# Rotary embedding: the half swap by DMA in place of a product with a sign matrix

## The chip, the cores and the metric

The kernel runs on one core of one Trainium2 chip. Five engines work beside each other, each through its own instructions in order: TensorE (PE in the profile) for matrix products, VectorE (DVE), ScalarE (ACT), GpSimd (POOL) and SyncE (SP), which here issues most of the DMAs. ACT and POOL issue some DMAs too. Tiles live in SBUF; matrix products go to PSUM. The metric is the device time of one execution in microseconds, as the median over several runs.

## What is computed

Two transformer blocks over 256 tokens of width 1024. The first has a convolution and Fourier mixer, attention over a memory and a mixture of experts. The second has two layers, each a mixer and an MLP; the change lies in its two mixers alone. Cut to what matters:

```python
def apply_rope(t, cos, sin):
    t1, t2 = jnp.split(t, 2, axis=-1)            # 64 wide: two halves of 32
    rot = jnp.concatenate([-t2, t1], axis=-1)
    return (t * cos + rot * sin).astype(t.dtype)

def mixer_ab(h, cos, sin, w_in, q_norm, w_uq, w_uiq, sinks, w_out):
    aq, ak, av, cq, bk, bv, bik, biw = _split_widths(h @ w_in, AB_WIDTHS)
    ...    # rope of aq and ak (8 and 2 heads), window attention
    cq = rms_norm(cq, q_norm)
    ...    # rope of bq = cq @ w_uq, biq = cq @ w_uiq, bk and bik
    yb = dsa_attention(bq, bk, bv, biq, bik, iw)   # top 64 keys by index scores
    return jnp.concatenate([ya, yb], axis=-1) @ w_out

def mixer_c(h, cos, sin, w_in, w_out):
    q, k, v = jnp.split(h @ w_in, 3, axis=-1)
    ...    # rope of q and k, 16 heads, causal attention
    return moba_attention(q, k, v) @ w_out
```

## The kernel before

Features stand on the partitions and tokens along a row, so a head of 64 takes 64 partitions and two heads a tile of 128. The half swap of rope is then a move across partitions: row `f` needs row `f + 32` with a minus sign, or row `f - 32`.

`rope()` takes a projection in PSUM (`pA`) and cuts it into pieces of 128 x 2 x 256, called raws below. ACT copies each piece to an SBUF tile `raw`, of which there are two. A function `rotate`, put off to the next `tick` or `drain`, multiplies `raw` on PE with the constant sign matrix `rot` into a PSUM tile `pB`; POOL writes `raw` times cosine to the result, DVE writes `pB` times sine over `raw`, and DVE adds the two.

There are 16 pieces. `mixer_ab` has four calls of two: `kd` (all keys), `iq` (index queries), `bq` and `aq` (queries of its two attentions). `mixer_c` has four groups of four heads, and each calls `rope` for `q` (the tile `cq__` with a number) and `k` (`ck`), one piece each.

Around them: matrix products are made of three terms (lines L394 to L396) from weights that are split into a high and a low part, `wh` by ACT (L192) and `wl` by DVE (L195). The weights come in 1 MB and 2 MB loads on SP's queue into rings of buffers, and a load can start when the split of the one before in its slot is done. In `mixer_ab`, `select` makes the index scores of 8 heads (`scores`, L1353 and L1354), ACT applies a relu to `rl`, DVE adds them up weighted in `acc` (L1479) and takes the top 64 in 8 rounds (MAX and MATCH_REPLACE). In the meantime PE works on `uq` and `ab_in`, the projections of `bq` and `aq`. In `mixer_c` the attention of a group runs along with the projections of the next: S and its softmax on DVE and ACT, its scaling on POOL (L1394), transposes on PE (L479), `PT` copies on ACT (L1405). `ada` products for the next norm are spread through both as fillers (`adasb`, L615 to L627, `mods`).

The order of each engine's instructions is fixed when the program is built: a scheduler goes by its own estimates of durations, and each engine then works its list in order, waiting on semaphores.

Of the kernel before, what the change touches and what calls it, by code (L numbers as in the profile page):

```python
# [17 lines left out]
T, D, E, FF = 256, 1024, 32, 4096  # L18
# [19 lines left out]
C_ID, C_UP, C_ROT, C_CAUS, C_WIN, C_IOTA, C_INV, C_ONES, C_SEL, C_SLOT, C_END = (  # L38
    0, 128, 256, 384, 768, 1152, 1216, 1217, 1345, 1346, 1347)
# [3 lines left out]
def constants():  # L43
    p = np.arange(128)
    c = np.zeros((128, C_END), np.float32)
    c[:, C_ID:C_UP] = np.eye(128)
    c[:, C_UP:C_ROT] = p[:, None] < p[None, :]
    for f in range(128):
        if f % 64 < 32:
            c[f + 32, C_ROT + f] = -1.0  # L50
        else:
            c[f - 32, C_ROT + f] = 1.0
# [159 lines left out]
class Net:  # L212
# [269 lines left out]
    def setup(self, ld):  # L482
# [11 lines left out]
        self.rot = cst[:, C_ROT:C_CAUS]  # L494
# [6 lines left out]
        self.slot = cst[:, C_SLOT:C_END]  # L501
# [76 lines left out]
    def angles(self, rp):  # L578
# [10 lines left out]
        for dst, turn in ((self.sin, 0.0), (self.cos, 0.25)):  # L589
# [10 lines left out]
            nc.scalar.activation(dst, r, AF.Sin)  # L600
# [816 lines left out]
    def mixer_ab(self, p, h, extra):  # L1417
# [28 lines left out]
        self.rope(p, pk, kd)  # L1446
# [16 lines left out]
        self.rope(p, self.fm_block("uiq", 0, cq, 2), iq)  # L1463
# [31 lines left out]
        self.rope(p, self.fm_block("uq", 0, cq, 2), bq)  # L1495
        self.rope(p, self.fm_block("ab_in", 0, h), aq)
# [181 lines left out]
```

## Time and profile before

| | us |
|---|---|
| median of 3 runs (lowest to highest) | 1852.88 (1852.48 to 1853.91) |
| the profiled execution | 1858.61 |
| its span, first to last instruction | 1856.8 |
| PE busy | 1729.1 |
| DVE busy | 940.0 |
| ACT busy | 565.0 |
| POOL busy | 141.8 |

Busy times are sums over one profiled execution, on engines that work at the same time. The mean granted clock of TensorE in it is 0.979 of full speed. A row of the trace gives an instruction with the line of the kernel, what it writes and reads, and in brackets how long its engine was idle ahead of it and which instruction ended the wait. Buffer numbers are left out of names, so `pB` stands for many PSUM tiles.

### The profile page before, as it was taken

How to read it: one execution, taken by the hardware profiler on the slowest of the kernel's cores; microseconds unless marked ns; L12 is line 12 of the kernel's file. 1: busy time of each engine (PE TensorE's matmuls, PEld its weight loads, DVE VectorE, ACT ScalarE, POOL GpSimd, SP SyncE). 2: the span in 40 equal slices, each digit the busy share in tenths (PEclk: the TensorE clock that was granted, in tenths of full speed). 3: DMA queues.
4: the chain of work that ended last, by engine and by line, in shares of the span. 5: the costliest groups of instructions: out<-in, count | busy, mean ns of one | idle time of the engine just before them, and what ended most of it. 6: DMA issues, size and time to landing. Idle time of an engine off the chain costs nothing. (4 is left out here: it accounts for less than half of the span.)

```text
span 1856.8 us, 24948 instructions
## 1 busy us (share of the span) xinstructions
PE 1729.1 (93%) x10060; PEld 1110.4 (60%) x10060; DVE 940.0 (51%) x1752; ACT 565.0 (30%) x1037; POOL 141.8 (8%) x113
## 2 busy tenths in 40 slices
PE   7999999999989989899899988898999989989997
PEld 7998844434433333333333333665899978869996
DVE  6777413232322323132222223578877699977555
ACT  6445421111111111111111110437444444544442
POOL 0000000000000000000000000223300033330001
PEclk9999999999999999999999999899999999999999
DMA  8685879999999999999999999836477748536540
GB/s 313 225 309 205 342 307 422 425 424 425 425 424 427 424 425 424 425 425 425 427 423 427 424 426 378 272 131 243 162 279 263 247 157 260 204 114 237 194 159 24
DMA packets 133492, 588.17 MB, mean 317 GB/s; under 512 B 13110, under 2 KB 37148, under 8 KB 100604
## 3 DMA queue, kind: packets, MB, share of 16 engines
q1 hardware_dynamic: 131756, 581.28, 79.7%
q0 software_dynamic: 1328, 4.72, 0.8%
q8 instruction: 81, 1.33, 0.3%
q10 hardware_dynamic: 288, 0.52, 0.1%
q14 instruction: 39, 0.32, 0.0%
HBM read 585.45 MB, written 1.05 MB: 316 GB/s over the span
## 5 line engine op out<-in xcount | busy, mean ns | idle before, releaser
L195 DVE TENSOR_TENSOR wl<-wa,wh 128x1024 fp32r<-128x1024 f32 (+1 forms) x244 | 304.6, 1260 | 138.8 <-ACT wh L192 133.8
L192 ACT ACTIVATE wh<-wa 128x1024 fp32r<-128x1024 f32 (+1 forms) x246 | 250.5, 1031 | 252.5 <-PE pA L395 114.6
L1067 PE MATMUL pA<-wb,xT 128*64 128x512 f32 x1024 | 236.2, 601 | 20.1 <-DMA wb<-in_w_gate_up_dram 19.4
L390 DVE SCALAR_TENSOR_TENSOR ydl<-pB,slotw,ydh 128x512 fp32r<-128x512 f32 x32 | 24.0, 750 | 340.2 <-ACT ydh L389 340.2
L1039 ACT ACTIVATE xT<-pB,vp 128x128 f32<-128x128 f32 x128 | 40.0, 363 | 483.8 <-PE pB L1036 483.8
L1067 PEld LDWEIGHTS pA<-wb,xT 128*64 128x64 f32 x1024 | 68.7, 137 | 162.2 <-issue 113.5
L395 PE MATMUL pB<-hTh,wl 128*128 128x256 f32 x528 | 149.2, 283 | 1.5 <-DVE wl L195 1.5
L394 PE MATMUL pB<-hTh,wh 128*128 128x256 f32 x528 | 149.0, 282 | 1.2 <-ACT hTh L683 1.2
L396 PE MATMUL pB<-hTl,wh 128*128 128x256 f32 x528 | 148.8, 283 | 1.1 <-DVE hTl L685 1.1
L1132 DVE TENSOR_TENSOR x<-pB,x 128x512 f32<-128x512 f32 x128 | 79.7, 683 | 132.2 <-PE pB L1130 132.2
L1093 DVE TENSOR_TENSOR v<-pB,bgu 128x256 f32<-128x256 f32 x128 | 48.1, 418 | 180.2 <-PE pB L479 180.2
L1067 PE MATMUL pA<-wa,xT 128*64 128x512 f32 x528 | 125.5, 600 | 1.0 <-DMA wa<-in_w_gate_up_dram 1.0
L396 PE MATMUL pA<-hTl,wh 128*128 128x256 f32 x384 | 111.4, 291 | 7.8 <-DVE hTl L685 7.5
L394 PE MATMUL pA<-hTh,wh 128*128 128x256 f32 x384 | 115.5, 301 | 1.5 <-ACT hTh L683 1.0
L1111 PE MATMUL pB<-wa,aT 128*64 128x512 f32 x496 | 114.5, 596 | 0.3 <-DMA wa<-in_w_down_dram 0.3
L395 PE MATMUL pA<-hTh,wl 128*128 128x256 f32 x384 | 111.1, 290 | 0.3 <-DVE wl L195 0.3
L627 DVE SCALAR_TENSOR_TENSOR adasb<-wa,silu,adasb 128x512 f32<-128x512 f32 x126 | 106.6, 846 | 1.8
L394 PE MATMUL pA<-wh,amh 128*128 128x512 f32 (+1 forms) x272 | 103.6, 381 | 0.0
L396 PE MATMUL pA<-wl,amh 128*128 128x512 f32 (+1 forms) x272 | 102.9, 378 | 0.0
L395 PE MATMUL pA<-wh,aml 128*128 128x512 f32 (+1 forms) x272 | 102.7, 378 | 0.0
L394 PEld LDWEIGHTS pB<-hTh,wh 128*128 128x128 f32 x528 | 100.0, 189 | 3.3 <-ACT hTh L683 2.8
L395 PEld LDWEIGHTS pB<-hTh,wl 128*128 128x128 f32 x528 | 100.1, 189 | 2.7 <-DVE wl L195 2.3
(357 smaller groups left out, 3037.6 us busy)
## 6 DMA issues: line engine op xcount, KB each, us to landing
wb<-in_w_gate_up_dram SPq DMA_DIRECT2D x64, 2048.0 KB
wa<-in_w_gate_up_dram SPq DMA_DIRECT2D x66, 1024.0 KB
wa<-in_mlp_w_dram SPq DMA_DIRECT2D x64, 1024.0 KB
wa<-in_w_down_dram SPq DMA_DIRECT2D x62, 1024.0 KB
wa<-in_ada_w_dram SPq DMA_DIRECT2D x48, 1024.0 KB
wb<-in_w_down_dram SPq DMA_DIRECT2D x21, 2048.0 KB
wd<-in_w_gate_up_dram SPq DMA_DIRECT2D x20, 2048.0 KB
wc<-in_w_gate_up_dram SPq DMA_DIRECT2D x11, 2048.0 KB
```

The lines of the kernel that those rows point to most:

```text
L192: nc.scalar.activation(h, a, AF.Copy)
L195: eng.tensor_tensor(l, a, h.bitcast(F32), OP.subtract)
L390: nc.vector.scalar_tensor_tensor(lo, src, scale, hi.bitcast(F32), op0=OP.mult, op1=OP.subtract)
L394: mm(out, lh, rh, start=start, stop=False, skip_group_check=True)
L395: mm(out, ll, rh, start=False, stop=False, skip_group_check=True)
L396: mm(out, lh, rl, start=False, stop=stop, skip_group_check=True)
L627: nc.vector.scalar_tensor_tensor(sb, v, c, sb, op0=OP.mult, op1=OP.add)
L1039: nc.scalar.activation(xT[:, k, :n], ps[:, j, :n], AF.Copy, scale=g[:, k:k + 1])
L1067: self.up = nc.tensor.matmul(gu[h * 64:h * 64 + 64, b, :], xT[:, k, c0:c0 + SLOTS], w[0][:, n:n + 512], start=k == 0, stop=k == 7)
L1093: nc.vector.tensor_tensor(v[:, :, h, :], ps.rearrange("p (j h s) -> p j h s", j=4, h=2)[:, :, h, :], bias[:, h * 8 + b * 4:h * 8 + b * 4 + ...
L1111: self.up = nc.tensor.matmul(dn[h * 64:h * 64 + 64, :], aT[:, k, :], w[0][:, h * 512:h * 512 + 512], start=k == 0, stop=k == 7)
L1132: nc.vector.tensor_tensor(xs, ps, xs, OP.add)
```

## The change

The sign matrix and its product are gone. ACT copies a piece from PSUM straight into its place in the result tile. Four DMAs, issued by ACT, copy its four blocks of 32 partitions to the partitions 32 away into a second tile: in `mixer_c` a tile `turned` of which there are two, in `mixer_ab` a part of one of the two `S` buffers of the attention (`shared`). POOL multiplies the piece by the cosine in place, DVE multiplies the turned one by the sine in place, and DVE adds them. The minus sign sits in the sine: its activation has a scale of -1 or +1 for each partition. There are 64 such DMAs of 64 KB.

```diff
--- before.py
+++ after.py
...
+    c[:, C_SIGN] = np.where(p % 64 < 32, -1.0, 1.0)
...
@@ -597,7 +593,10 @@
             if turn:
                 nc.vector.tensor_scalar(r, r, math.pi / 2, None, op0=OP.add)
             nc.vector.tensor_scalar(r, r, 3.1415925, -3.1415925, op0=OP.min, op1=OP.max)
-            nc.scalar.activation(dst, r, AF.Sin)
+            if turn:
+                nc.scalar.activation(dst, r, AF.Sin)
+            else:
+                nc.scalar.activation(dst, r, AF.Sin, scale=self.sign)
             yield
@@ -1325,26 +1324,29 @@
                         out(n, z, mv[:, t, 0:1], rs[:, t:t + 1])
         return finish
 
-    def rope(self, p, ps, out):
+    def rope(self, p, ps, out, shared=False):
 
         nc = self.nc
         nb = ps.shape[1]
-        raw = p.tile([128, 2, T], F32, name="raw", bufs=2)
-        raws = [raw]
-        for j in range(0, nb, 2):
-            if j:
-                raws.append(p.tile([128, 2, T], F32, name="raw", bufs=2))
-            nc.scalar.activation(raws[-1], ps[:, j:j + 2, :], AF.Copy)
+        raws = [out[:, j:j + 2, :] for j in range(0, nb, 2)]
+        for j, raw in enumerate(raws):
+            nc.scalar.activation(raw, ps[:, 2 * j:2 * j + 2, :], AF.Copy)
+        if shared:
+            turned = p.tile([128, 4, 384], F32, name="S", bufs=2)[:, :nb, :T]
+        else:
+            turned = p.tile([128, nb, T], F32, name="turned", bufs=2)
+        for j, raw in enumerate(raws):
+            for i in range(4):
+                a, b = i * 32, (i ^ 1) * 32
+                nc.scalar.dma_start(turned[a:a + 32, 2 * j:2 * j + 2, :], raw[b:b + 32])
         sinb, cosb = (x[:, None, :].to_broadcast([128, 2, T]) for x in (self.sin, self.cos))
 
         def rotate():
             for i, raw in enumerate(raws):
-                r = self.B()
-                nc.tensor.matmul(r, self.rot, raw.rearrange("p k t -> p (k t)"), start=True, stop=True)
-                o = out[:, 2 * i:2 * i + 2, :]
-                nc.gpsimd.tensor_tensor(o, raw, cosb, OP.mult)
-                nc.vector.tensor_tensor(raw, r.rearrange("p (k t) -> p k t", k=2), sinb, OP.mult)
-                nc.vector.tensor_tensor(o, o, raw, OP.add)
+                r = turned[:, 2 * i:2 * i + 2, :]
+                nc.gpsimd.tensor_tensor(raw, raw, cosb, OP.mult)
+                nc.vector.tensor_tensor(r, r, sinb, OP.mult)
+                nc.vector.tensor_tensor(raw, raw, r, OP.add)
         self.soon.append(rotate)
 
     def scores(self, q, k):
@@ -1443,7 +1445,7 @@
         nc.scalar.activation(sq, pc, AF.Square)
         for f in range(2):
             self.evac_hl(pc[:, f, :], cq[0][:, f, :], cq[1][:, f, :], self.col["ab_q_norm_2"][:, f:f + 1])
-        self.rope(p, pk, kd)
+        self.rope(p, pk, kd, True)
         rs = p.tile([128, 2], F32, name="trs")
         rs8 = p.tile([128, 2], F32, name="rs8")
         iw = p.tile([128, 2, 8], F32, name="iw")
...
```

The rest of the diff takes the sign matrix out of the constants, and gives `True` for `shared` in the four calls of `mixer_ab`.

The change also moves instructions. Three places follow, as the lists of the engines stand before and after, in each list's own line numbers.

On DVE, at the start of the index selection of `mixer_ab`, from the first sine product of `iq` on, stands before:

```order
L1346 TENSOR_TENSOR raw_8007<-pB_8021,sin_96 128x512
L1458 TENSOR_SCALAR rs8_7943<-trs_7942 128x2
L1460 TENSOR_SCALAR iw_7944<-vt_7928,trs_7942 128x8 x2
L1347 TENSOR_TENSOR iq_7945<-iq_7945,raw_8007 128x512
L1346 TENSOR_TENSOR raw_8009<-pB_8026,sin_96 128x512
L1347 TENSOR_TENSOR iq_7945<-iq_7945,raw_8009 128x512
L1479 SCALAR_TENSOR_TENSOR acc_8031<-rl_8035,iw_7944,cst_73 128x128
L1479 SCALAR_TENSOR_TENSOR acc_8031<-rl_8035,iw_7944,cst_73 128x256
L1479 SCALAR_TENSOR_TENSOR acc_8031<-rl_8042,iw_7944,acc_8031 128x128
L1479 SCALAR_TENSOR_TENSOR acc_8031<-rl_8042,iw_7944,acc_8031 128x256
```

and now:

```order
L1348 TENSOR_TENSOR S_8012<-S_8012,sin_96 128x2x256
L1349 TENSOR_TENSOR iq_7952<-iq_7952,S_8012 128x512
L1481 SCALAR_TENSOR_TENSOR acc_8037<-rl_8041,iw_7951,cst_73 128x128
L1481 SCALAR_TENSOR_TENSOR acc_8037<-rl_8041,iw_7951,cst_73 128x256
L1348 TENSOR_TENSOR S_8012<-S_8012,sin_96 128x2x256
L1481 SCALAR_TENSOR_TENSOR acc_8037<-rl_8048,iw_7951,acc_8037 128x128
L1349 TENSOR_TENSOR iq_7952<-iq_7952,S_8012 128x512
L1481 SCALAR_TENSOR_TENSOR acc_8037<-rl_8048,iw_7951,acc_8037 128x256
```

The two halves of `iq` were done ahead of the first sum into `acc`. Now the second half's sine product and sum stand between the sums into `acc`, and the first sine product of `bq` (not shown) stands ahead of the last pair of these, where it was behind the whole selection.

On ACT, in `mixer_ab` from the copies of `kd` (two rows of `raw`) past those of `iq`, with the semaphores on which each waits (PE, DVE and Activation are engines, DMAHW with a digit one of eight counters on which DMAs of SP and ACT end in turn), stands before:

```order
L1337 ACTIVATE raw<-pA 128x512 [waits PE_49]
L1337 ACTIVATE raw<-pA 128x512
L1443 ACTIVATE sqc<-pB 128x512 [waits PE_49]
L389 ACTIVATE cqh<-pB,v_89 128x256
L192 ACTIVATE wh<-wa 128x1024 [waits DVE_49,PE_49]
L1440 ACTIVATE vt<-pB 128x400 [waits PE_49]
L389 ACTIVATE cqh<-pB,v_89 128x256 [waits DVE_49]
L1337 ACTIVATE raw<-pA 128x512 [waits DVE_49,PE_49] x2
L1477 ACTIVATE rl<-pB 128x384 [waits PE_49] x2
L1477 ACTIVATE rl<-pB 128x384 [waits DVE_49,PE_49,Activation_49] x6
```

and now, from the first `cqh` on:

```order
L385 ACTIVATE cqh<-pB,v_89 128x256
L1341 DMA S<-kd 32x2x256 [waits Activation_49]
L385 ACTIVATE cqh<-pB,v_89 128x256 [waits DVE_49]
L1442 ACTIVATE vt<-pB 128x400 [waits PE_49]
L1341 DMA S<-kd 32x2x256 x2
L1341 DMA S<-kd 32x2x256 [waits DMAHW6_49]
L1341 DMA S<-kd 32x2x256 [waits DMAHW7_49,Activation_49]
L1341 DMA S<-kd 32x2x256 [waits DMAHW0_49]
L1341 DMA S<-kd 32x2x256 [waits DMAHW1_49]
L1341 DMA S<-kd 32x2x256 [waits DMAHW2_49]
L188 ACTIVATE wh<-wa 128x1024
L1333 ACTIVATE iq<-pA 128x512 [waits PE_49]
```

The DMAs of `kd` now stand ahead of the split `wh` and the copies of `iq`; five of them wait for the counter that an earlier DMA holds.

On DVE, in the second group of `mixer_c`, around its two ropes, from the reciprocal of the group before on, stands before:

```order
L1391 RECIPROCAL sm<-sm 128x4 [waits Activation_49]
L1346 TENSOR_TENSOR raw<-pB,sin 128x512 [waits PE_49,Pool_49]
L195 TENSOR_TENSOR wl<-wa,wh 128x1024 [waits DMAHW4_49,Activation_49]
L1347 TENSOR_TENSOR cq__11160<-cq__11160,raw 128x512 [waits DVE_49]
L627 SCALAR_TENSOR_TENSOR adasb<-wa,silu,adasb 128x512
L627 SCALAR_TENSOR_TENSOR adasb<-wa,silu,adasb 128x512 [waits DVE_49]
L195 TENSOR_TENSOR wl<-wa,wh 128x1024 [waits PE_49,Activation_49]
L387 TENSOR_TENSOR oTl<-pB,oTh 128x256 [waits Activation_49] x2
L1346 TENSOR_TENSOR raw<-pB,sin 128x512 [waits PE_49,Pool_49]
L195 TENSOR_TENSOR wl<-wa,wh 128x1024 [waits DMAHW6_49,Activation_49]
L1347 TENSOR_TENSOR ck<-ck,raw 128x512 [waits DVE_49]
```

and now:

```order
L1393 RECIPROCAL sm<-sm 128x4 [waits Activation_49]
L191 TENSOR_TENSOR wl<-wa,wh 128x1024 [waits PE_49,Activation_49]
L1348 TENSOR_TENSOR turned<-turned,sin 128x512 [waits DMAHW3_49,DMAHW7_49,DMAHW1_49,DMAHW0_49]
L191 TENSOR_TENSOR wl<-wa,wh 128x1024 [waits DMAHW4_49,Activation_49]
L1349 TENSOR_TENSOR cq__11176<-cq__11176,turned 128x512 [waits DVE_49,Pool_49]
L383 TENSOR_TENSOR oTl<-pB,oTh 128x256 [waits Activation_49]
L1348 TENSOR_TENSOR turned<-turned,sin 128x512 [waits DMAHW6_49,DMAHW7_49,DMAHW5_49,DMAHW0_49]
L1349 TENSOR_TENSOR ck<-ck,turned 128x512 [waits DVE_49,Pool_49]
L383 TENSOR_TENSOR oTl<-pB,oTh 128x256 [waits Activation_49]
L191 TENSOR_TENSOR wl<-wa,wh 128x1024
L191 TENSOR_TENSOR wl<-wa,wh 128x1024 [waits Activation_49]
```

The sine products waited for PE's product and for POOL's; now each waits for four DMAs, and the sums wait for POOL. The fillers `adasb` that stood between are now ahead, and the product of `ck` stands between the two `oTl`.

## Rows read from the trace of the kernel before

**Rows 1.** The page's part 1: busy time, share of the span, instructions.
```profile
PE 1729.1 (93%) x10060; PEld 1110.4 (60%) x10060; DVE 940.0 (51%) x1752; ACT 565.0 (30%) x1037; POOL 141.8 (8%) x113
```

**Rows 2.** Windows: length, then busy of PE, PEld, DVE, ACT, POOL; clock, DMA share, GB/s.
```profile
1195.00:1210.00 15.00, 15.00 (x131) 13.96 (x133) 6.13 (x5) 7.00 (x9) 0.65 (x1) 1.00 0.90 308
1220.00:1230.00 10.00, 9.46 (x68) 7.45 (x67) 9.12 (x25) 4.80 (x10) 2.16 (x3) 1.00 0.00 1
1527.00:1632.00 105.00, 102.55 (x788) 91.52 (x786) 98.92 (x144) 52.95 (x118) 33.26 (x22) 1.00 0.70 232
```

**Rows 3.** Timeline of PE in mixer_ab: start us, us, instruction, [idle <-releaser].
```profile
1214.74 1.88 PE L1343 MATMUL pB<-raw,cst 128*128 128x512 f32 x4
...
1216.46 0.95 PE L638 MATMUL pB<-cst,adasb 128*128 128x1 f32 x8
...
1218.16 0.37 PE L394 MATMUL pA<-cqh,wh 128*128 128x256 f32 x1
...
1222.72 0.50 PE L1353 MATMUL pB<-kd,iq 64*128 64x128 f32 x4 [0.46 <-DVE iq L1347]
```

**Rows 4.** Timeline of DVE in mixer_ab: start us, us, instruction, [idle <-releaser].
```profile
1224.18 0.75 DVE L1479 SCALAR_TENSOR_TENSOR acc<-rl,iw,cst 128x128 f32<-128x128 f32 x2 [0.27 <-ACT rl L1477]
...
1239.06 0.68 DVE L1346 TENSOR_TENSOR raw<-pB,sin 128x512 f32<-128x512 f32 x1
1239.65 0.35 DVE L1490 TENSOR_SCALAR acc<-acc 128x384 f32<-128x384 f32 x1
...
1243.58 0.69 DVE L1346 TENSOR_TENSOR raw<-pB,sin 128x512 f32<-128x512 f32 x1 [1.18 <-POOL aq L1345]
...
1246.59 1.01 DVE L1368 SCALAR_TENSOR_TENSOR S<-pB,cst 128x384 f32<-128x384 f32 x2
```

**Rows 5.** Lines L1343 and L1346: count, ns min/median/max, first and last start.
```profile
L1343 PE MATMUL pB<-raw,cst x32: 590/592/697, 1214.7 to 1618.5; 128*128 128x512 f32 x32
L1346 DVE TENSOR_TENSOR raw<-pB,sin x16: 655/682/693, 1215.9 to 1619.2; 128x512 f32<-128x512 f32 x16
```

**Rows 6.** Timeline of ACT in mixer_ab, ahead of the iq copies.
```profile
1211.80 0.51 ACT L389 ACTIVATE cqh<-pB,v 128x256 fp32r<-128x256 f32 x1
1217.38 0.60 ACT L1337 ACTIVATE raw<-pA 128x512 f32<-128x512 f32 x1 [5.08 <-DVE kd L1347]
```

**Rows 7.** The tile out_dram: DMA issues, count, ns min/median/max, first and last start.
```profile
L1644 ACTq DMA_DIRECT2D out_dram<-n x2: 338/358/377, 1847.6 to 1852.9; - x2
L1602 SPq DMA_DIRECT2D out_dram<-n x2: 351/356/361, 1851.8 to 1853.5; - x2
```

**Rows 8.** DMA issues: form, count, KB each, median us from issue to landing.
```profile
gb<-in_norm_final_dram POOLq DMA_DIRECT2D x1, 512.0 KB, 10.8
```

**Rows 9.** Windows around an idle stretch of PE, columns as in group 2.
```profile
1254.00:1260.00 6.00, 1.99 (x18) 0.91 (x10) 5.97 (x21) 4.15 (x18) 2.34 (x4) 1.00 0.86 332
1260.00:1264.00 4.00, 4.00 (x22) 2.21 (x22) 2.26 (x11) 3.21 (x13) 2.63 (x4) 0.58 0.11 7
```

**Rows 10.** Waits from 1527 to 1650 us: us in total, times, longest.
```profile
DVE raw L1346 <- PE pB L1343: 2.9, 3, 1.6
PE pB L479 <- POOL S L1394: 2.8, 2, 1.5
```

**Rows 11.** Line L1347, the sum on DVE: count, ns min/median/max, starts.
```profile
L1347 DVE TENSOR_TENSOR ck<-ck,raw x4: 681/684/684, 1544.7 to 1620.0; 128x512 f32<-128x512 f32 x4
L1347 DVE TENSOR_TENSOR aq<-aq,raw x2: 691/866/1041, 1244.3 to 1246.0; 128x512 f32<-128x512 f32 x2
L1347 DVE TENSOR_TENSOR cq__10860<-cq__10860,raw x1: 1791/1791/1791, 1537.9 to 1537.9; 128x512 f32<-128x512 f32 x1
L1347 DVE TENSOR_TENSOR cq__11160<-cq__11160,raw x1: 1524/1524/1524, 1561.7 to 1561.7; 128x512 f32<-128x512 f32 x1
```

**Rows 12.** Timeline of POOL, two of its cosine products.
```profile
1241.85 2.95 POOL L1345 TENSOR_TENSOR aq<-raw,cos 128x512 f32<-128x512 f32 x2 [9.72 <-ACT raw L1337]
...
1537.70 1.42 POOL L1345 TENSOR_TENSOR ck<-raw,cos 128x512 f32<-128x512 f32 x1 [2.64 <-ACT raw L1337]
```

More of the change, by code (lines that the diff above doesn't have):

```diff
@@ L36 @@
 FILL_LI = (0,)
-C_ID, C_UP, C_ROT, C_CAUS, C_WIN, C_IOTA, C_INV, C_ONES, C_SEL, C_SLOT, C_END = (
-    0, 128, 256, 384, 768, 1152, 1216, 1217, 1345, 1346, 1347)
+C_ID, C_UP, C_ROT, C_CAUS, C_WIN, C_IOTA, C_INV, C_ONES, C_SEL, C_SLOT, C_SIGN, C_END = (
+    0, 128, 256, 256, 640, 1024, 1088, 1089, 1217, 1218, 1219, 1220)
 D_BLK, D_COS, D_SIN, D_END = 0, 256, 768, 1280
@@ L47, in constants @@
     c[:, C_UP:C_ROT] = p[:, None] < p[None, :]
[L48 to L52, printed above, removed]
     tri = np.where(p[None, :] <= p[:, None], 0.0, NEG)
@@ L493, in setup @@
         self.upper = cst[:, C_UP:C_ROT]
-        self.rot = cst[:, C_ROT:C_CAUS]
         self.caus = cst[:, C_CAUS:C_WIN]
@@ L500, in setup @@
         self.sel4 = cst[:, C_SEL:C_SLOT]
-        self.slot = cst[:, C_SLOT:C_END]
+        self.slot = cst[:, C_SLOT:C_SIGN]
+        self.sign = cst[:, C_SIGN:C_END]
         self.mhalf = per.tile([128, 1], F32, name="mhalf")
@@ L1462, in mixer_ab @@
         iq = p.tile([128, 4, T], F32, name="iq")
-        self.rope(p, self.fm_block("uiq", 0, cq, 2), iq)
+        self.rope(p, self.fm_block("uiq", 0, cq, 2), iq, True)
         token_scale()
@@ L1494, in mixer_ab @@
         bq = p.tile([128, 4, T], F32, name="bq")
-        self.rope(p, self.fm_block("uq", 0, cq, 2), bq)
-        self.rope(p, self.fm_block("ab_in", 0, h), aq)
+        self.rope(p, self.fm_block("uq", 0, cq, 2), bq, True)
+        self.rope(p, self.fm_block("ab_in", 0, h), aq, True)
         self.drain()
```

## The prediction

> **What bounds the kernel now.** I read the page's first part first: TensorE (PE) is busy in 93% of the span and VectorE (DVE) in 51% [rows 1]. That speaks for any change that takes work from PE, so the next question is whether PE is the limit where this work lies. The windows answer by stage [rows 2]. The four calls of `mixer_ab` lie between 1207 and 1247 us, the eight of `mixer_c` between 1527 and 1632 us. In `mixer_c` PE is busy for 102.55 of 105 us, but DVE for 98.92 of the same 105: PE is first, and DVE only 3.6 us behind.
>
> In `mixer_ab` the timeline of PE has a wait of 0.46 us for DVE at the first scores, at 1222.72 [rows 3], so PE goes at DVE's pace there. DVE's own timeline [rows 4] shows the reason: the first `acc` of the selection starts at 1224.18, and from there DVE works without a gap (the MAX and MATCH_REPLACE rounds lie between the rows shown) to the first sine product of `bq` at 1239.06. It ends the two `bq` halves, waits 1.18 us for POOL's cosine product of `aq`, and starts the attention's S at 1246.59. This chain sets the stage's end; PE's 96 matmuls of `ab_in` lie beside it.
>
> **What is removed.** 32 records of the sign product. Their duration is 592 ns, but they overlap: four take 1.88 us [rows 3, 5], 0.47 each, so 32 x 0.47 = 15.0 us of PE, half in each mixer. ACT's 5.08 us wait before the raw copy of `iq` [rows 6] goes too. The 16 sine products on DVE stay (655 to 693 ns), and so do the sums, POOL's products and ACT's copies.
>
> **What is added: 64 DMAs of 64 KB.** *Issue.* The trace has two DMAs issued by ACT, 338 to 377 ns each [rows 7]. I take 0.36: four cost 1.4 us of ACT's queue, and 32 in a mixer 11.5. In `mixer_c` ACT is busy 52.95 of 105 us, so there is room, except for what stands right behind them. *Landing.* No transfer inside SBUF is in the trace. The lower bound is the last output DMA, 256 KB, issued at 1853.5 with the span's end at 1856.8: 3.3 us. The upper one is a 512 KB load on POOL's queue, 10.8 us [rows 8]. The new ones are a quarter of the smaller of these, so I take 3.3 and keep 10.8 as the end of the range. *Lanes.* As the order shows, several of the new DMAs wait on the semaphore of an earlier transfer of SP's. Those transfers are the 1 MB `ada` loads, issued while the stage runs; what stands behind a waiting DMA on ACT are the copies of `iq` and the weight split `wh`.
>
> **mixer_ab, step by step.** Without sign products PE goes from `uiq`, which ended at 1214.74, through 16 short matmuls (they held it from 1216.46 to 1218.16, 1.7 us), 24 of `uq` and 52 of `ab_in` to the scores. A window full of such matmuls has 131 in 15.00 us, 0.115 each [rows 2], so 76 take 8.7 and the scores come at 1225.1, 2.4 later than before. Is `iq` ready? ACT's work ahead of it ended at 1212.3 [rows 6]; eight `kd` DMAs add 2.9 (1215.2), the `iq` copies 1.1, four DMAs 1.4 (1217.7). They land at 1221.0, sine product and sum take 1.3: 1222.3. So 2.8 us of PE's other matmuls cover the landing; one of 6.1 instead of 3.3 uses that up, and one of 10.8 makes the scores 4.7 us later.
>
> DVE's chain is then: first `acc` 2.4 later; the sine product and sum of the second `iq` half and the first sine product of `bq` now stand inside the selection, three operations at 0.6 each (the next instruction started 0.59 after the product at 1239.06) [rows 4], +1.85 with a little over the 1.77 for the wait between product and sum. Behind it, `bq` has one product less (-0.59), the wait for POOL goes since `aq` is copied long before (-1.18), and the sum of `aq` that took 1.04 beside POOL takes 0.69 as the other did (-0.35) [rows 11]. Sum: 2.4 + 1.85 - 0.59 - 1.18 - 0.35 = **+2.1**. Where PE's 7.5 us go: into idle time before the attention, since `ab_in` ends before the selection does. The trace shows what follows idle PE: of 1254 to 1260 it is busy 1.99 us at full clock, and in the 4 us behind it the granted clock is 0.58, which is 1.2 instead of 2.4 GHz for most of them [rows 9]. The attention's start then runs slow, as in part it did already; DVE paces it, so I take +0.5, with 0 and 2 (half of such a stretch) as ends. `mixer_ab`: **+2.6**, from 0 to +4.1 without late landings.
>
> **mixer_c.** PE's stream shortens by 7.5 to 95.1 of 105 us. Of that, the transposes' waits for POOL's S (2.8 us in two waits) [rows 10] come earlier and so give some back: PE alone would allow -6.5. DVE is then the longer one. Its 98.92 us hold 8 sine products that read PSUM; now they read two SBUF tiles and start with POOL's cosine product, since one landing releases both. The rows show the difference: at 1243.58 a sine product from PSUM took 0.69 [rows 4] while POOL worked on `aq` from 1241.85 for 2.95 us [rows 12]; at 1537.9 a sum of two SBUF tiles took 1.79, where the four of `ck` take 0.68 [rows 11], and it ran beside POOL's product of `ck` [rows 12]. So each product costs from 0 to 1.1 more. In return the sums, of which two of eight were stretched before (1.79 and 1.52) [rows 11], come after POOL is done. I take 0.4 for each of 8, +3.2: DVE at 102.1. DVE's 2.9 us of waiting for the sign product [rows 10] go, and waits for landings of `ck`, whose DMAs stand behind a PT copy on ACT, come in their place. So the stage cannot shrink by more than 105 - 102.1 = 2.9 unless DVE's share of the extra cost is hidden; I take **-2.5**, from -6.5 (PE alone) to +3 (DVE at 98.92 + 8 x 1.1 = 107.7).
>
> The Trainium skill has a rule for these rows ("SBUF — State Buffer", section Who interferes with whom): a DVE instruction with two SBUF inputs contends with a GpSimd instruction that reads SBUF, and one with at most one SBUF input does not. By it this change turns eight instructions per mixer from the free kind into the other, which speaks against it; the trace agrees with it, 0.69 against 1.79 [rows 4, 11].
>
> Moved early work (the sine's sign, a `w_gate_up` load some issues earlier) I put at 0: the same instructions at the same lengths, in another order.
>
> **Sum.** +2.6 - 2.5 = +0.1. The profiled execution has 1858.61 us, with 1856.8 from first to last instruction; it would be 1858.7. The median of the runs is 5.7 lower, 1852.88, so the forecast is **1853.0**.
>
> **Rivals.**
> 1. *PE's saving in `mixer_c` counts in full.* For it: PE is busy 97.7% there and waits for DVE little. Against it: DVE's 98.92. Then -6.5 + 2.6 = -3.9: 1849.0, and 1846.4 without a loss in `mixer_ab`.
> 2. *Slower: DVE becomes the bound of `mixer_c`.* If each sine product runs beside POOL's and is stretched like the sum at 1537.88, DVE needs 107.7 of 105 us: +2.7, with `mixer_ab` +5.3: 1858.2; a wait of 1 us for the landing of `ck` in three groups makes it 1861.2. The point from which it decides: 0.9 us more for each product make 98.92 + 7.2 = 106.1, +1.1, and with +2.6 the 3.7 us that count as slower. The skill's rule named above is this rival's mechanism; by it the time is 1858.2.
> 3. *Late `iq`.* A landing of 10.8 us in `mixer_ab` (behind the `ada` loads on the same lanes): +4.7 + 2.6 - 2.5 = +4.8: 1857.7. Against it: the DMA share is 0.00 from 1220 to 1230 [rows 2], so the loads in front have landed by then.
> 4. *All of PE's 15.0 us count.* 1837.9. Against it speaks the unbroken DVE chain of `mixer_ab`.
>
> **Chances.** Forecast (between -3.7 and +3.7) 0.40; rival 1 0.29; rivals 2 and 3 together 0.29 (2: 0.21, 3: 0.08); rival 4 0.02. About 0.2%, 3.7 us, is what a measurement of this kernel tells from no change: faster means under 1849.2, slower over 1856.6. So faster 0.31, same 0.40, slower 0.29. The range for 8 in 10 reaches from rival 1 without loss to rival 2 with its landings: 1846.4 to 1861; the forecast's own is 1849.2 to 1856.6.
>
> **What would show it.** Right: from 1207 to the attention's first S (1246.59 before) some 2 us more, the first `acc` near 1226.6, PE idle for over 8 us ahead of the scores of `aq`; in `mixer_c` a stretch of 102 to 103 us where it had 105, sine products with a mean over 0.9 us, DVE busy above 97% of it. Rival 1 shows sine products near 0.7 and a stretch under 99.5. Rival 2 shows them above 1.4, PE waiting for `wl`, and more than 106 us. Rival 3 shows PE waiting for `iq`, and landings above 5 us. What would make it wrong beyond that is a wait of ACT's queue for a lane ahead of the exponentials in `mixer_c`: all that ACT issues stands behind it.

## The result, and the profile after

The changed kernel takes 1872.91 us in the median of 4 runs (1869.74 to 1874.43). The kernel before took 1853.39 on the same chip. The ratio is 1.0102 with a 95% interval of 1.009 to 1.0114: 19.5 us slower, outside the forecast's range. The profiled execution took 1869.74 us, with a span of 1867.8.

The page's part 1 of the changed kernel, which answers to [rows 1]: PE has 8.5 us less to do and the span is 11 us longer.
```profile
PE 1720.6 (92%) x10028; PEld 1105.4 (59%) x10028; DVE 938.3 (50%) x1752; ACT 564.2 (30%) x1037; POOL 144.7 (8%) x113
```

Windows of the changed kernel (columns as in [rows 2]). The first three lie in `mixer_ab`, the others in `mixer_c`; the fourth is the stretch of [rows 2] at the same distance from the stage's start.
```profile
1220.00:1235.00 15.00, 10.99 (x73) 9.35 (x72) 11.60 (x22) 3.98 (x9) 2.67 (x2) 0.77 0.32 93
1240.00:1250.00 10.00, 0.00 (x0) 0.00 (x0) 10.00 (x38) 1.88 (x2) 5.61 (x2) 0.55 0.40 131
1250.00:1260.00 10.00, 9.77 (x64) 4.68 (x64) 7.88 (x25) 3.12 (x13) 1.50 (x2) 0.77 0.48 151
...
1533.11:1638.11 105.00, 97.55 (x737) 89.44 (x736) 86.81 (x127) 47.29 (x101) 29.26 (x20) 0.93 0.74 234
...
1548.00:1555.00 7.00, 4.98 (x23) 4.98 (x24) 4.46 (x8) 1.11 (x2) 1.70 (x1) 0.51 1.07 320
1555.00:1582.00 27.00, 24.73 (x203) 22.46 (x203) 20.28 (x32) 13.49 (x31) 9.56 (x6) 1.00 0.64 196
1582.00:1589.00 7.00, 7.00 (x38) 6.35 (x36) 7.00 (x16) 2.92 (x9) 0.35 (x1) 0.52 0.52 155
```
In `mixer_c` PE and DVE both have gaps now, 97.55 and 86.81 us busy of 105 where it was 102.55 and 98.92: neither is the bound, something is waited for. Twice 7 us run at about half clock, 1.2 instead of 2.4 GHz.

DVE's timeline in `mixer_ab` after the change (answers to [rows 4]):
```profile
1214.90 0.69 DVE L1348 TENSOR_TENSOR S<-S,sin 128x512 f32<-128x512 f32 x1 [1.89 <-DMA S<-kd]
1216.77 1.77 DVE L1349 TENSOR_TENSOR kd<-kd,S 128x512 f32<-128x512 f32 x1 [1.18 <-POOL kd L1347]
1218.47 2.31 DVE L191 TENSOR_TENSOR wl<-wa,wh 128x1024 fp32r<-128x1024 f32 x1
1220.70 1.75 DVE L1348 TENSOR_TENSOR S<-S,sin 128x512 f32<-128x512 f32 x1
...
1223.95 0.69 DVE L1349 TENSOR_TENSOR iq<-iq,S 128x512 f32<-128x512 f32 x1
1226.89 0.75 DVE L1481 SCALAR_TENSOR_TENSOR acc<-rl,iw,cst 128x128 f32<-128x128 f32 x2 [2.26 <-ACT rl L1479]
...
1231.82 3.22 DVE L1481 SCALAR_TENSOR_TENSOR acc<-rl,iw,acc 128x128 f32<-128x128 f32 x6 [0.94 <-ACT rl L1479]
...
1251.21 0.69 DVE L1349 TENSOR_TENSOR aq<-aq,S 128x512 f32<-128x512 f32 x1 [1.17 <-POOL aq L1347]
1251.85 1.02 DVE L1370 SCALAR_TENSOR_TENSOR S<-pB,cst 128x384 f32<-128x384 f32 x2
```
DVE waits for `kd`'s landing, then for POOL, and the three instructions behind that take 1.75 to 2.31 us. POOL's timeline shows its cosine products beside all three:
```profile
1214.94 3.05 POOL L1347 TENSOR_TENSOR kd<-kd,cos 128x512 f32<-128x512 f32 x2 [2.39 <-DMA S<-kd]
1217.96 1.74 POOL L1347 TENSOR_TENSOR iq<-iq,cos 128x512 f32<-128x512 f32 x1
1220.52 1.37 POOL L1347 TENSOR_TENSOR iq<-iq,cos 128x512 f32<-128x512 f32 x1 [0.83 <-DMA S<-iq]
1233.47 1.30 POOL L1347 TENSOR_TENSOR bq<-bq,cos 128x512 f32<-128x512 f32 x1 [11.58 <-DMA S<-bq]
```
So `iq`, which DVE's list puts after `kd`, is ready only at 1224.6. PE's timeline shows who waits:
```profile
1224.69 0.80 PE L1355 MATMUL pB<-kd,iq 64*128 64x128 f32 x4 [4.01 <-DVE iq L1349]
...
1250.19 0.80 PE L1355 MATMUL pB<-kd,aq 64*128 64x128 f32 x4 [12.88 <-DVE aq L1349]
```
The last POOL row meets DVE too. The first line below is the sum into `acc` that runs beside it, the second gives the fourteen such sums of before (ns min/median/max), the third POOL's two products of `aq`:
```profile
L1481 DVE SCALAR_TENSOR_TENSOR acc<-rl,iw,acc x1: 1555/1555/1555, 1233.5 to 1233.5; 128x256 f32<-128x256 f32 x1
```
```profile
L1479 DVE SCALAR_TENSOR_TENSOR acc<-rl,iw,acc x14: 347/414/480, 1224.8 to 1229.3; 128x128 f32<-128x128 f32 x7, 128x256 f32<-128x256 f32 x7
```
```profile
L1347 POOL TENSOR_TENSOR aq<-aq,cos x2: 1262/3392/5522, 1244.3 to 1245.7; 128x512 f32<-128x512 f32 x2
```
The sum takes 1.56 us, where none took more than 0.48 before. POOL's first product of `aq`, beside the last MAX rounds, takes 1.26 us, the second 5.52: beside that one DVE works on products and sums without a gap until 1250.04, and it ends 1.1 us later. In these rows the two engines hold each other up both ways.

ACT's timeline, with the DMAs it issues:
```profile
1207.88 4.23 ACTq L1341 DMA_DIRECT2D S<-kd  x6
1212.16 1.06 ACT L188 ACTIVATE wh<-wa 128x1024 fp32r<-128x1024 f32 x1 [4.35 <-issue]
...
1213.74 5.18 ACTq L1341 DMA_DIRECT2D S<-iq  x8
...
1229.62 0.49 ACT L1479 ACTIVATE rl<-pB 128x384 f32<-128x384 f32 x1 [1.37 <-DMA S<-bq]
1231.30 0.49 ACT L1479 ACTIVATE rl<-pB 128x384 f32<-128x384 f32 x1 [1.19 <-PE pB L1356]
...
1535.50 3.33 ACTq L1341 DMA_DIRECT2D turned<-cq__10872  x4
...
1542.78 3.74 ACTq L1341 DMA_DIRECT2D turned<-ck  x4
```
The wait of `wh` for "issue" is the time of the six DMAs ahead of it on ACT's queue.

DVE and PE in `mixer_c` after the change, first and second group (two timelines):
```profile
1545.00 0.69 DVE L1348 TENSOR_TENSOR turned<-turned,sin 128x512 f32<-128x512 f32 x1 [1.48 <-DMA turned<-cq__10872]
1545.61 2.30 DVE L191 TENSOR_TENSOR wl<-wa,wh 128x1024 fp32r<-128x1024 f32 x1
...
1552.51 0.69 DVE L1348 TENSOR_TENSOR turned<-turned,sin 128x512 f32<-128x512 f32 x1 [1.41 <-DMA turned<-ck]
...
1578.44 0.69 DVE L1348 TENSOR_TENSOR turned<-turned,sin 128x512 f32<-128x512 f32 x1 [2.16 <-DMA turned<-ck]
1580.29 0.69 DVE L1349 TENSOR_TENSOR ck<-ck,turned 128x512 f32<-128x512 f32 x1 [1.16 <-POOL ck L1347]
```
```profile
1550.02 1.86 PE L637 MATMUL pB<-cst,adasb 128*128 128x1 f32 x8 [3.91 <-DVE adasb L626]
...
1581.13 0.50 PE L1355 MATMUL pB<-ck,cq__11176 64*128 64x128 f32 x4 [2.27 <-DVE ck L1349]
```
The four DMAs of `ck` were issued by 1546.5 and DVE could start at 1552.5, 6 us later. The first half-clock window above begins within PE's first wait (1546.1 to 1550.0), the second just behind its second.

**Stages against their own start.** Because single executions differ, I compare starts within a stage. The first table gives, for `mixer_ab`, the start of a row less that of the second POOL `rs<-rs` (1170.83 in the changed kernel), in us; "unchanged" is the mean of the five experiments below that leave `mixer_ab` alone (e2, e8, e11, e14, e16), whose first scores differ by 1.6 and whose ends by 1.1. The profiled execution of before had a stretch at half clock ahead of the rope (0.51 from 1182 to 1192), has its first scores at 52.4 and its end at 140.65, and is left out here. Those of e10 and e19 had the same stretch (0.50 from 1180 to 1190 and from 1182 to 1192), which puts some 3.8 us into each of their columns: read these two rows by the differences within them.

| kernel | first `iq` scores | first `acc` | first MAX | `aq` scores | attention's S | first `lrs` (end) |
|---|---|---|---|---|---|---|
| unchanged | 48.6 | 50.1 | 55.6 | 71.4 | 72.5 | 136.3 |
| changed | 53.9 | 56.1 | 65.4 | 79.4 | 81.0 | 146.2 |
| e1 | 52.7 | 54.2 | 62.5 | 77.5 | 79.1 | 144.3 |
| e13, `kd` by product | 49.1 | 50.6 | 58.9 | 74.5 | 76.2 | 142.5 |
| e10, `bq`, `aq` by DMA | 52.4 | 53.9 | 59.4 | 80.7 | 82.3 | 150.4 |
| e12, no swap | 49.9 | 53.5 | 59.0 | 74.7 | 75.9 | 139.7 |
| e19, idle filled | 55.9 | 57.4 | 66.6 | 84.1 | 85.0 | 149.1 |

The second gives the first scores of the four groups of `mixer_c` and its end, less the start of the second `lrs` before it.

| kernel | group 1 | 2 | 3 | 4 | end |
|---|---|---|---|---|---|
| e1 (`mixer_c` unchanged) | 34.7 | 59.0 | 85.3 | 111.1 | 140.6 |
| changed | 38.7 | 63.9 | 92.9 | 118.7 | 147.1 |
| e14, `k` by DMA | 38.4 | 65.1 | 92.6 | 119.7 | 150.2 |
| e11, `q` by DMA | 35.5 | 60.5 | 85.2 | 109.9 | 140.7 |
| e3, no swap | 35.3 | 59.3 | 84.5 | 108.2 | 139.6 |

### The profile page after: what moved, and what is told of

Read it like the earlier page. It is cut to its first block, busy times and chain, and to the rows that moved or that the text cites. A ratio compares the mean times of both kernels' runs of the same rounds, so it can differ in the third digit from the quotient of the medians.

```text
span 1867.8 us, 25001 instructions
## 1 busy us (share of the span) xinstructions
PE 1720.6 (92%) x10028; PEld 1105.4 (59%) x10028; DVE 938.3 (50%) x1752; ACT 564.2 (30%) x1037; POOL 144.7 (8%) x113
```

## Experiments

Three theories stood at the start: the transfers land too late (A), POOL and DVE hinder each other (B), or the issues hold up ACT's queue (C). Two came later: the changed order of the lists costs by itself (D), or PE's idle time does, through the clock behind it (E). Differences are medians against the kernel before, run on the same chip; intervals are those of the ratio. A function `rope_mm` is the old `rope`, with the sign in the sine. Most diffs below are against the changed kernel, and leave out what gives the matrix its place in the constants.

**Each mixer alone.**
```diff
+        if not shared:          # e1; e2 has "if shared:"
+            return self.rope_mm(p, ps, out)
```


> The DMAs in mixer_ab alone; mixer_c goes back to a product on PE (a plain swap matrix, since the sign stays in the sine). In the traces mixer_ab lost some 10 us from the copy of kd to the end of the stage, mixer_c some 5. Theory A (the turned half comes late: four issues of 0.6 us on ACT's queue, waits for a lane, landings of some 6 us beside the weight loads, and DVE, POOL and PE wait in order behind it) and theory B (POOL's and DVE's products start together on one landing and block each other) both expect two thirds of the 19.5 us here: +10 to +15. A theory that PE's falling clock or another run-wide effect makes the loss expects no such split, say +17 or more or under +5.

> The DMAs in mixer_c alone; mixer_ab goes back to a product on PE. Theories A and B: +4 to +8, and the sum with the run of mixer_ab alone is 17 to 22. If the two are not additive (sum under 12 or over 27), something outside of the two stages, such as the order of the loads, carries part of the loss.

e1: 1863.22 us, +9.8 (1.0062, 1.004 to 1.0084). e2: 1858.6, +5.1 (1.0031, 1.0019 to 1.0044). Both mixers lose. Together that is 14.9 of 19.5, less than the 17 to 22 expected, but the ratios add up to 1.0093 against 1.0102, which the intervals cover.

**No swap at all (e3), and in `mixer_ab` alone (e12).**
```diff
-                nc.scalar.dma_start(turned[a:a + 32, 2 * j:2 * j + 2, :], raw[b:b + 32])
...
-                nc.vector.tensor_tensor(r, r, sinb, OP.mult)
+                nc.vector.tensor_tensor(raw, raw, sinb, OP.mult)
```


> Neither product nor DMA: the half swap is left out, DVE multiplies the copied piece itself by the sine. This is the change with a swap that costs nothing. Theory A: the loss was the way of the turned half, so this is faster than before by what PE's saving is worth, -3 to -8 us. Theory B: the products with two SBUF inputs beside POOL remain, and so does a good part of the loss: 0 to +10.

> The half swap left out in mixer_ab alone (neither product nor DMA there, DVE multiplies the copied piece itself by the sine), mixer_c with a product. The run without any swap was +8.4, its trace showed +2.9 in mixer_ab and -1 to -2.7 in mixer_c. Theory D (what the freed PE does to the order and to PE's idle time costs by itself): +3 to +6. Theories A and B without D: -2 to +1.

e3: 1861.86, +8.4 (1.0049, 1.0032 to 1.0066). e12: 1860.17, +7.3 (1.004, 1.0022 to 1.0059). So without a single DMA the kernel is already slower, and nearly all of that is `mixer_ab`. DVE's timeline of e12 shows a product of `bq` ahead of the first `acc`, waiting for POOL:
```profile
1216.02 1.46 DVE L1484 TENSOR_SCALAR iw<-vt,trs 128x8 f32<-128x8 f32 x2
...
1221.34 1.74 DVE L1348 TENSOR_TENSOR raw<-raw,sin 128x512 f32<-128x512 f32 x1 [1.47 <-POOL bq L1347]
1223.00 0.73 DVE L1503 SCALAR_TENSOR_TENSOR acc<-rl,iw,cst 128x128 f32<-128x128 f32 x2
```
That is the 3.7 us from scores to `acc` in the table, where 1.5 stood. This product runs beside POOL's second product of `bq` and takes 1.74 us instead of 0.69; `iw`, beside POOL's products of `iq`, takes 1.46, where the changed kernel has 0.36. So e12 takes the DMAs away, but neither the new order nor POOL's work beside DVE, and it does not tell theory D from theory B. In `mixer_c`, e3 has the last scores 2.9 us earlier than e1 but the end only 1.0: that much a free swap is worth there.

**DMAs without a use (e4): the kernel before, with 64 more that copy constants.**
```diff
+                nc.scalar.dma_start(turned[a:a + 32, j:j + 2, :], self.cst[b:b + 32, :512 if shared else T].rearrange("p (k t) -> p k t", k=2))
```


> The kernel before with its product on PE, and beside it 64 DMAs that nobody reads, issued by ACT at the same places (four per piece, source a constant; 64 KB each in mixer_ab, 32 KB in mixer_c). Theory A: issue and lanes on ACT cost something by themselves, but nobody waits for a landing: +1 to +5. A theory C, that ACT's queue is the loss (64 issues of 0.6 us and their lane waits delay the exponentials and the splits behind them): +10 to +20. Theory B: 0 to +3.

1870.41, +17 (1.0091, 1.0074 to 1.0108). It doesn't tell the theories apart as meant: nothing holds these DMAs back, so the scheduler put them early, ahead of weight splits and the `cqh` copies on ACT, and PE waited there:
```profile
PE pA L394 <- ACT cqh L389: 11.4, 1, 11.4
```
It shows that DMAs on ACT's queue cost much where they stand ahead of what PE waits for.

**Other queues and fewer DMAs: POOL's (e5), the two pieces of a call of `mixer_ab` in one DMA (e6), SP's (e7), POOL's in `mixer_c` alone (e8).**
```diff
-                nc.scalar.dma_start(turned[a:a + 32, 2 * j:2 * j + 2, :], raw[b:b + 32])
+                nc.gpsimd.dma_start(turned[a:a + 32, 2 * j:2 * j + 2, :], raw[b:b + 32])   # e5, e8
+                nc.sync.dma_start(turned[a:a + 32, 2 * j:2 * j + 2, :], raw[b:b + 32])     # e7
+            nc.scalar.dma_start(turned[a:a + 32, :, :], out[b:b + 32])                     # e6
```


> The changed kernel with its 64 DMAs issued by POOL in place of ACT. ACT's queue is free of them, and they no longer wait for counters that SP's loads hold; the landing itself stays. Theory C (ACT's queue: 0.6 us for each issue and the waits for counters, with wh, relu and the exponentials behind them): the loss falls from +19.5 to what remains with a swap that costs nothing, +5 to +11. Theory A (the landing beside the loads is late, whoever issues): +15 to +22. POOL's own cosine products stand behind the issues now, up to 0.6 us each: both theories allow 2 us for it.

> The changed kernel with one DMA for both pieces in mixer_ab: 16 of 128 KB there in place of 32 of 64 KB; mixer_c unchanged. Theory C: half of the issues and counter waits of the stage go, some 10 us of ACT's queue, and 2 to 6 us of the loss with them: +13 to +17. Theory A: landings don't come earlier, the first half of a call even waits for the second copy: +18 to +21.

> The changed kernel with its 64 DMAs issued by SP, between the weight loads. ACT is free of them, but the waits for counters stay and now hold up SP's loads instead. Theory C with the issue time as its core: +6 to +12. Theory C with the counter waits as its core, or theory A: +15 or more, and a load that comes late behind them would show as PE waiting for a DMA.

> The DMAs in mixer_c alone, issued by POOL (mixer_ab as with a product on PE). Issued by ACT this cost +5.1. Theory C: -3 to +2, since without the way of the turned half mixer_c gains some 2.7 us in the trace without a swap. Theory A: +4 to +8.

e5 +27.7 (1.0157, 1.0137 to 1.0178), e6 +15.9 (1.0092, 1.0075 to 1.0109), e7 +15.2 (1.0084, 1.0067 to 1.0101), e8 +12.9 (1.0072, 1.0053 to 1.009; e2, the same on ACT, +5.1). Freeing ACT's queue gives back some 4 us at most, and the intervals of e6 and e7 overlap that of the changed kernel, so ACT's issue time is not the main cause; on POOL, which also has the cosine products, it is worse than any theory expected. In e7 the first `iq` scores still come 55.9 us into the stage, 7.3 later than unchanged.

**POOL's product out of place in `mixer_ab` (e9), so that it need not wait for the landing.**
```diff
+        raws = [p.tile([128, 2, T], F32, name="raw", bufs=2) for j in range(0, nb, 2)]
...
+                nc.gpsimd.tensor_tensor(o, raw, cosb, OP.mult)
```


> The DMAs in mixer_ab alone (as in the run that cost +9.8), but ACT copies each piece to a tile of its own and POOL writes the cosine product to the result, as before the change: POOL no longer waits for the DMAs and does not start together with DVE's sine product. Theory B (the two products block each other): +4 to +7, DVE's products back at 0.7 us. Theory A (late landing of kd ahead of iq): +8 to +11, since DVE waits for the landing as before.

1862.0, +9.2 (1.0052, 1.0032 to 1.0072), as e1. `iq` was done at 1221.1 instead of e1's 1223.8, but ACT then waited for a `raw` tile until DMAs had read it, and for the issue of seven DMAs:
```profile
1215.39 0.60 ACT L1338 ACTIVATE raw<-pA 128x512 f32<-128x512 f32 x1 [1.12 <-DMA S<-raw]
...
1220.10 0.60 ACT L1338 ACTIVATE raw<-pA 128x512 f32<-128x512 f32 x1 [4.11 <-issue]
```
One wait took the other's place. DVE's stretched rows remain as well: a sum of `kd` takes 1.75 us, a sine product 1.78 and a sum into `acc` 1.51, so e9 did not take POOL from DVE's side and does not exclude theory B.

**Which of the four ways in `mixer_ab`: only `bq` and `aq` by DMA (e10), all but `kd` (e13).**
```diff
-        self.rope(p, pk, kd, True)
+        self.rope(p, pk, kd)                                            # e10, e13: without True, by product
-        self.rope(p, self.fm_block("uiq", 0, cq, 2), iq, True)
+        self.rope(p, self.fm_block("uiq", 0, cq, 2), iq)                # e10
```


> DMAs for bq and aq alone, whose landing has over 5 us before anyone needs it; kd and iq and all of mixer_c by a product. Theory A: the loss of mixer_ab (+9.8) lies in kd and iq, so it goes: -1 to +3. A theory D, that the loss comes from PE running ahead and then standing still before the attention (clock), or from the order of DVE's list: +5 or more. Theory B: +1 to +4, as POOL's products of bq fall among DVE's sums.

> In mixer_ab kd goes back to a product, iq, bq and aq stay with DMAs; mixer_c by a product. With all four by DMA this cost +9.8, with bq and aq alone +12.1. Theory A (kd lands late, beside the ada loads, and DVE and POOL stand in order behind it, so that iq is late at the scores): PE's 2.8 to 4.0 us wait for iq goes and the cost falls to +3 to +6. If it stays at +8 or more, what the freed PE does to the order of the lists (theory D) carries mixer_ab.

e10: 1864.92, +12.1 (1.0055, 1.0035 to 1.0076); e13: 1863.85, +10.4 (1.0055, 1.0039 to 1.0071). Theory A expected +3 to +6 for e13 and -1 to +3 for e10, and misses both. In e13 the scores come at 49.1, so `kd`, ahead of `iq` in DVE's list, was what made `iq` late. But the kernel is no faster for it than e1: from `acc` to MAX it takes 8.3 us (5.5 unchanged), and from the attention's S to the end 66.3 (63.8 unchanged). In e10 DVE and PE wait for `aq` in turn:
```profile
1244.85 0.69 DVE L1353 TENSOR_TENSOR S<-S,sin 128x512 f32<-128x512 f32 x1 [4.35 <-DMA S<-aq]
1246.70 1.73 DVE L1354 TENSOR_TENSOR aq<-aq,S 128x512 f32<-128x512 f32 x1 [1.15 <-POOL aq L1352]
```
```profile
1248.58 0.80 PE L1382 MATMUL pB<-kd,aq 64*128 64x128 f32 x4 [10.54 <-DVE aq L1354]
```

**Which of the two ways in `mixer_c`: only `q` by DMA (e11), only `k` (e14), `q` from the second group on (e16).**
```diff
-            self.rope(p, self.fm_group("c_in", g * 256, h), q)
-            self.rope(p, self.fm_group("c_in", 1024 + g * 256, h), k)
+            self.rope(p, self.fm_group("c_in", g * 256, h), q, g == 0)      # e16 (True: by product); e11: unchanged; e14: True
+            self.rope(p, self.fm_group("c_in", 1024 + g * 256, h), k, True)  # e11, e16; e14: unchanged
```


> DMAs for q of mixer_c alone; k of mixer_c and all of mixer_ab by a product. With both by DMA this cost +5.1. Theory A: the short way is that of k (its DMAs are issued last and PE's scores wait for ck), so q alone costs -2 to +2, apart from the first group, where q landed late beside full loads. If q costs +3 or more, it is not the scores' wait but DVE's, which stands in order behind a late landing wherever it is.

> DMAs for k of mixer_c alone; q there and all of mixer_ab by a product. Both cost +5.1, q alone +0.4. Theory A (the exposed way is that of k, whose copy comes last before the scores): +4 to +6. If it is under +2, the cost is that of 8 DMAs a group in a row on ACT and of two landings close together, not that of k's own way.

> The part of the change that should be worth keeping: DMAs for q of mixer_c in the groups 2 to 4 alone, whose landing has a group's projections of k and v to hide behind; the first q, which landed late beside full loads, and all else by a product. Theory A: three products fewer, 1.4 us of PE at most: -2 to 0. A theory that any of these DMAs costs more than the product it replaces: +1 or more.

e11: 1853.27, +0.4 (1.0006, 0.9996 to 1.0016). e14: 1860.68, +7.2 (1.004, 1.0026 to 1.0054). e16: 1852.12, -1.4 (0.9985, 0.9975 to 0.9995). In `mixer_c` these three have one buffer each of `turned` and `raw`, where e2 has two of `turned` and e1 two of `raw`. The swap of `q` is hidden, that of `k` is not: the scores need `k` right behind its projection, and in e14 DVE waits at the first group:
```profile
1541.64 0.69 DVE L1353 TENSOR_TENSOR turned<-turned,sin 128x512 f32<-128x512 f32 x1 [3.51 <-DMA turned<-ck]
```
e16 is faster than both kernels by its interval, though by less than the 0.2% that a single comparison tells.

**Idle time filled: matmuls that nothing reads, in e13 (e17), e12 (e18) and the changed kernel (e19).**
```diff
+                if r >= 4:
+                    ps = self.B()
+                    for t in range(2):
+                        nc.tensor.matmul(ps[:8, :], m8[:, t, :], self.cst[:, :512], start=True, stop=True)
...
+            ps = self.B()
+            for t in range(2):
+                nc.tensor.matmul(ps, acc[:, :128], self.cst[:, :512], start=True, stop=True)
```


> The kernel of e13 (in mixer_ab the decay keys keep the product, the three other ways go by DMA; mixer_c with products) with matmuls added that nothing reads, issued by TensorE from the selection rounds on, where e13 shows it idle ahead of the attention of the selected keys. Theory E (the loss is TensorE standing idle ahead of that attention, after which the attention starts at half clock): the granted clock behind 1245 us stays near full and the run falls from e13's +10.4 us to about +4 us over the kernel before. Theory D (the loss is the changed order on TensorE's list and the late swapped rows, whatever the clock does): within 2 us of e13, +8.4 to +12.4.

> The kernel of e12 (the swap of the halves is left out in mixer_ab, neither product nor DMA, sign in the sine; mixer_c with products) with the same unread matmuls from the selection rounds on. Theory E: from e12's +7.3 us to about +2 us, with a clock near full behind 1245 us. Theory D: within 2 us of e12, +5.3 to +9.3.

> The changed kernel with the same unread matmuls in mixer_ab; mixer_c as changed. Theory E: from +19.5 us to about +14 us, the gain all in mixer_ab. Theory D: within 2 us of the changed kernel, +17.5 to +21.5.

The kernel before had 1854.89 here. e17: 1874.99, +20.1 (1.0117, 1.0082 to 1.0151); e18: 1867.54, +12.7 (1.0068, 1.0052 to 1.0085); e19: 1869.55, +14.7 (1.0079, 1.0061 to 1.0096). e17 and e18 say nothing on the clock: the added matmuls moved the last projection of `aq` behind them in PE's list, so its copy comes late. ACT in e17 (e13 has it at 1233.27):
```profile
1245.66 1.08 ACT L1338 ACTIVATE aq<-pA 128x512 f32<-128x512 f32 x2 [17.20 <-PE pA L394]
```
In e19 `aq` stays in place, and the windows show the attention's start at full clock, where the changed kernel has 0.77:
```profile
1240.00:1250.00 10.00, 8.28 (x14) 1.53 (x15) 8.40 (x36) 0.00 (x0) 2.53 (x2) 0.67 0.17 39
1250.00:1260.00 10.00, 9.11 (x60) 3.60 (x59) 7.81 (x19) 3.26 (x8) 0.00 (x0) 1.00 0.46 147
```
Its ratio is 0.0023 under that of the changed kernel, as theory E expected (about 4 us), but the two intervals overlap, and the profile does not show the gain where E puts it. From S to the end it has 64.1 us against 65.2, 1.1 of the 4; from MAX to the scores of `aq`, where the added matmuls stand ahead of these on PE, it takes 3.5 us more; and `mixer_c`, which e19 leaves as it was, takes 145.5 us in it against 147.1. So E is not shown.

## Why the prediction was wrong

**mixer_ab, forecast +2.6, measured +9.8 (e1).** In the profile of the changed kernel it is +9.9. Step by step, by the first table:
- *The scores, +2.4 forecast, +5.2 measured.* PE did arrive early, at 1220.7, but waited 4.01 us. The step that failed is "Is `iq` ready?": it counted ACT and the landing, took DVE as free, and put the stretch of DVE's instructions beside POOL, which it priced in `mixer_c`, at nothing here. DVE works its list in order, and `kd` stands ahead of `iq` there: a wait of 1.89 for `kd`'s landing, 1.18 for POOL, and 3.2 us more than without POOL beside it (1.77, 2.31 and 1.75 against 0.69, 1.23 and 0.69). Rival 3 had the place (late `iq`, +4.7) but not the cause: `iq`'s own landing was not the last thing. e13 shows the place: with `kd` by product the scores lose 0.5. It shows as well that the whole does not hang on it, since e13 costs +10.4.
- The Trainium skill has the rule for those 3.2 us ("SBUF — State Buffer", section Who interferes with whom: a DVE instruction with two SBUF inputs contends with a GpSimd instruction that reads SBUF). The trace agrees, and also shows that it strikes whatever stands there, such as the split `wl` (2.31 us), and not the changed products alone.
- *Three products inside the selection, +1.85 forecast; from `acc` to MAX +3.8 measured.* The three are there. Of the other 2 us, 1.1 are the one sum into `acc` that runs beside POOL's product of `bq` (1.56 us instead of 0.48), again the stretch that the prediction left out here. The other 0.9 are DVE's wait for `rl` at 1231.82; that relu (1231.30) had waited for PE's scores, which stood behind projections that ran at half clock. The issues of `bq`'s DMAs between the relus held up ACT (1.37 us at 1229.62), but DVE has no wait there.
- *Behind it, -2.1 forecast, -1.9 measured* from MAX to the scores of `aq`: right up to there. But the wait of 1.18 for POOL did not go, as forecast; it moved behind these scores (1.17 at 1251.21), since POOL's second product of `aq` took 5.52 us beside DVE.
- *Half clock, +0.5 forecast.* PE's idle time is there as forecast, 12.88 us. The three pieces left are 0.7 from the first scores to `acc`, 0.6 from the `aq` scores to S and 1.4 from S to the end; the windows show 0.77 of the clock over the first (1220 to 1235) and over the start of the attention (1250 to 1260). In the second piece DVE's sum of `aq`, late by the wait for POOL, ends as S starts, so the rows do not tell that wait from the clock.

These sum to 5.2 + 3.8 - 1.9 + 2.7 = 9.8. The first step was missed; in the second and the last the mechanism was right and the size off. In the first two, 1.18 + 3.2 + 1.1 = 5.5 us are time that DVE lost to POOL, more than the 1.9 of the landing. That a swap without DMAs loses too (e12) fits this. PE's 7.5 us had no use in this stage, as the prediction said, yet taking them away changed the scheduler's lists, and DVE's chain got more ahead of `acc` and beside POOL. How much of the loss is the order and how much is POOL is not shown: no run takes POOL's products from DVE's side. In e12's profile the loss is 3.3 us, in its median 7.3; e12's profiled execution was its shortest of five (1856.14, clock 0.980, up to 1863.1 at 0.975), so the other 4 go with the clock and stay unexplained beyond that.

**mixer_c, forecast -2.5, measured +5.1 (e2).** In the profile of the changed kernel it is +6.5 against e1. DVE was to be the longer engine through stretched sine products. They are not: six of the eight take 0.68 to 0.69 us and two 1.10 and 1.21, and DVE is busy 86.81 of 105 us. The stretch beside POOL hits the instruction behind the product instead, such as the split of 2.30 us at 1545.61. Rival 2 falls with that, though its sum (1858.2 to 1861.2) was the nearest on the slower side. The step that failed is the sentence on landings, which named the waits for `ck` and set them against the 2.9 us of waiting that go, without a price of their own. Landing takes 6 us beside the weight loads, not 3.3, and issuing four takes 3.3 and 3.7 in the first group, not 1.4 (four at 0.6 are 2.4, the rest is waiting between them). In the first group DVE waits for `cq`, its next split runs 2.30 beside POOL, the fillers behind it are late, and PE waits 3.91 for them; the group's scores come 4.1 later. At the second group PE waits 2.27 for `ck`. With each wait come 7 us at 0.51 and 0.52 of the clock, and the third group is another 2.8 later. e11 and e14 show that it is `k`: +0.4 against +7.2. They have other lists, though: the first group comes 0.8 later in e11 and 3.7 in e14, where PE waits 2.25 for `ck` itself and not for fillers.

**The cost of an issue**, 0.36 forecast from 128-partition writes, was 0.6. By e6 and e7 it is a small part of the loss, at most some 4 us of 19.5.

**Open.** How much of `mixer_ab`'s loss is POOL beside DVE (B), how much the order (D) and how much the clock (E); and 4 us of e12. The 4.6 us between the sum of e1 and e2 and the whole are within the intervals.

## What to carry to other kernels

A transfer that takes work off the busiest engine pays only where that engine is waited for at this place and the result is not needed soon: here `q` had such slack and `k`, `kd` and `aq` did not. When pricing it, follow the in-order list of the engine that consumes the first transfer, since whatever stands behind it inherits the wait. Look also at what runs beside it on the other engines: a product that starts at another time can meet and slow an instruction that was not changed, as POOL's did with the split `wl`. And leave out the transfer altogether in one run: if the kernel is slower even so, a faster transfer will not give that part of the loss back.

## What was not expected of the hardware

These DMAs between partitions of SBUF cost more to issue than the output's DMAs to DRAM ([rows 7], 338 to 377 ns). The tile `S` of the changed kernel, and `turned` of e5 on POOL:
```profile
L1341 ACTq DMA_DIRECT2D S<-kd x8: 593/607/754, 1205.2 to 1211.5; - x8
```
```profile
L1341 POOL DMA_DIRECT2D turned<-ck x16: 496/500/532, 1548.4 to 1638.3; - x16
```
On SP it was 585 to 595 ns in the median (e7). And 64 KB needed 6 us to land while loads held the DMA share at 1.07. Where less else moved it was shorter: in e5 the trace has the landings (the last number, us from issue to landing):
```profile
S<-kd POOLq DMA_DIRECT2D x8, 64.0 KB, 6.3
S<-bq POOLq DMA_DIRECT2D x8, 64.0 KB, 1.9
```
The DMA share was 1.01 from 1206 to 1217, around those of `kd`, and 0.30 from 1224 to 1232, around those of `bq`. So the 3.3 us of the forecast lie between the two.
